# A hybrid decoder layer on one core: descriptor scratch of 4 KB, rows of inverse roots by two float32r products, and the norms of one k group four slots later

## The chip, the cores and the metric

The kernel runs on one core of a Trainium2 chip. The metric is the time of one execution on the device in microseconds, as the median of several runs. A profiled execution of the same program gives the trace. Its engines are TensorE (PE, with its weight loads shown apart as PEld), VectorE (DVE), ScalarE (ACT), GpSimd (POOL) and SyncE (SP); each takes its own queue of instructions in order. Transfers are issued by SyncE's queue (weights, transposes, results) and by GpSimd's (transfers that add to what lies at their target).

## The reference

One decoder layer for 512 tokens of 2048 channels, all in float32, with weights of 2048 x 7168, 1024 x 1024 and 2048 x 2048:

```python
h = rms_norm(x, norm_g)
a_val, a_glu, a_gate, q, k, v, b_gate = jnp.split(h @ w_in, SPLIT_POINTS, axis=-1)   # 1024 columns each
u = a_val * jax.nn.sigmoid(a_glu)
u = causal_depthwise_conv(u, conv_w, conv_b)                                      # 31 taps
u = jax.nn.silu(layer_norm(u, conv_norm_g, conv_norm_b))
y_a = (u @ conv_pw_w + conv_pw_b) * jax.nn.silu(a_gate)
q, k = rms_norm(q, q_norm_g), rms_norm(k, k_norm_g)                               # per head, 16 heads of 64
y_b = dilated_attention_mixture(q, k, v) * jax.nn.silu(b_gate)
out = x + jnp.concatenate([y_a, y_b], axis=-1) @ w_out
```

## The kernel before, in words

Activations lie with channels on the partitions and the 512 tokens along the free axis; q, k and v come out with tokens on the partitions. Weights come as *units* of 512 rows by 512 columns (1 MB), eight in flight (RING), and four (or fewer) units make a *group*: vg0 to vg3 (value and gate of the GLU), q0, k0, v0, bg0, q1, k1, v1, ag0, ag1, bg1, then the pointwise groups pw0 and pw1, then the output's wb and wa groups.

**Precision.** Almost every product is made of three float16 products (`tri`, L409 on): both operands are split into a high and a low float16 half, and high x high, high x low and low x high are summed. ScalarE rounds the high half (wh), VectorE subtracts it for the low half (wl). The first two groups (vg0, vg1) use a split into two float32r numbers instead (`exact_matmuls`, L876). Weights are scaled by a power of two; ScalarE finds a bound for it by squaring a whole unit into a tile that nobody reads (`junk`, in `row_squares`, L191) and summing, TensorE and VectorE sum it up, and GpSimd takes the inverse root by a power (`rsqrt`, L169, called from L205 on).

**Slots.** The order of all work is written by the program. A *slot* is a piece of TensorE's queue: six matmuls of 512 columns, eight slots to a unit. A calendar (`after(n, fn)`) puts work n slots ahead, and at each slot the program issues the work that is due, then convolution steps, then the matmuls. So the slot says where an instruction stands in each engine's queue, not when it runs.

**Seven products.** Groups vg3 and v0 (`SEVEN`) and the output's wa groups are computed as two by two blocks with seven products in place of eight. Such a group (`input_products`) needs sums of weight blocks: s1 is subtracted by VectorE, and s3, s2 and s4 (`BY_DMA`) are added by transfers from GpSimd's queue within the weights' own tiles (wf<-wf, L1119; in the output stage L933), 512 KB for each of two *pairs*. In a SEVEN group the program puts s2 at steps 3 and 4, s4 at 8 and 9; s2 reads what s3 made, s4 reads what s2 made, pair by pair. The step of a SEVEN group has 12 matmuls of 256 columns, and after its last step the next group's first weights are split (`split_hi`, `split_lo`). The transfers' descriptors lie in a scratch area whose size is an argument of the program, `dynamic_dma_scratch_size`.

**Convolution and layer norm.** The 31 taps run on VectorE as filler: at each slot `run_conv` issues convolution steps as long as VectorE's counted load stays under a pace, PACE before attention and PACE_2 once the first pair of heads has begun. The layer norm follows (`conv`, L534 on): a product with ones for the mean (L565), the centred squares, then `token_rsqrt` (L386 on), which makes a row of inverse roots by token on all partitions. It sums over channels with four small products (L390) into a column per 128 tokens, GpSimd takes the inverse roots of the 128 x 4 numbers, and the row has to be spread to all partitions. For the layer norm (n == C) this goes by DRAM: one transfer writes the 512 numbers (`by_token`, L396), a second reads them back to 128 partitions (`lnrow`, L397). For the first norm, over x, four diagonals are made on VectorE and one float32 product with ones gives the row (`rrow`, L400 to L406). Then, seven slots on, VectorE scales the eight channel tiles by the row (cv), ScalarE applies SiLU, and u is split for the pointwise products. The small products of the layer norm wait until a pair of heads is at least eight slots old.

**Norms of q and k.** `norm_qk` (L470 on) has four steps per tile of 128 tokens, at slots n after the tile has left PSUM: VectorE sums the squares by head (ss) and GpSimd takes the roots; VectorE scales z; ScalarE rounds the high half (qhl); VectorE subtracts, and SyncE's queue issues two transposing transfers. For k0 the steps of its four tiles fall around the start of v0, the SEVEN group behind it. Attention begins at the earliest 28 slots after k's last slot, at a multiple of eight slots from the start plus two.

## Time and profile before

| | |
|---|---|
| median of 3 runs | 831.17 us (830.96 to 832.64) |
| the profiled execution | 832.49 us |
| its span, first to last instruction | 830.6 us |
| granted clock of TensorE, mean | 0.997 |
| busy, share of the span: TensorE, VectorE, ScalarE, GpSimd | 98%, 83%, 66%, 15% |
| transfers | 122.71 MB, mean 148 GB/s |

All rows of the trace are of that one execution, and its times count from the span's start. A row of the timeline or the chain begins with the start in us and the length in us; in square brackets stand the engine's idle time before the instruction and what ended it. L80 is the line of a helper that all VectorE instructions go through, so they are told apart by their tiles. A row with x and a count is a group of instructions: busy time of all, mean of one in ns, and idle time ahead of them.

### The profile page before, as it was taken

What the parts mean: (1) busy time and instruction counts of PE and PEld (TensorE: products, weight loads), DVE (VectorE), ACT (ScalarE), POOL (GpSimd) and SP (SyncE); (2) the same over time, 40 slices, a digit from 0 to 9 for tenths busy, and PEclk for the clock granted to TensorE, in tenths of its full rate; (3) what the DMA queues carried; (4) which work ended last, traced back from release to release, by engine and by line L of the source; (5) the groups of instructions that cost most, each with busy time, mean ns of one, the idle gap of its engine ahead of it and who ended that gap; (6) DMA issues with size and microseconds to landing.
All of it is one profiled execution on the core that took longest, in us unless ns stands there. A gap on an engine that the chain in (4) does not pass through costs nothing.

```text
span 830.6 us, 13114 instructions
## 1 busy us (share of the span) xinstructions
PE 815.7 (98%) x5125; PEld 488.0 (59%) x5125; DVE 690.4 (83%) x1150; ACT 547.0 (66%) x768; POOL 124.2 (15%) x154
## 2 busy tenths in 40 slices
PE   9999999989999999999999999999998999999998
PEld 6787645854445864444444444444444444688887
DVE  6758989879897889999899898977367798888885
ACT  6667677465655579677666839578677948766541
POOL 0001022200514300003203010000210002232320
PEclk9999999999999999999999999999999999999999
DMA  9852243773392792627473642635344297579662
GB/s 339 336 209 102 101 128 77 138 217 109 107 193 55 148 253 102 165 102 165 133 151 113 163 128 79 149 101 155 102 109 120 92 225 249 125 173 190 115 123 69
DMA packets 95310, 122.71 MB, mean 148 GB/s; under 512 B 62416, under 2 KB 80592, under 8 KB 86032
## 3 DMA queue, kind: packets, MB, share of 16 engines
q1 hardware_dynamic: 80544, 107.37, 42.3%
q0 software_dynamic: 14416, 14.42, 12.2%
q8 instruction: 40, 0.66, 0.3%
q14 instruction: 22, 0.18, 0.1%
q10 hardware_dynamic: 288, 0.07, 0.0%
HBM read 88.82 MB, written 4.20 MB: 112 GB/s over the span
## 4 chain that ended last, share of the span: by engine, by line
PE 82%; DVE 5%; DMA 5%; issue 3%; ACT 2%; POOL 2%; SPq 0%; POOLq 0%; ACTq 0%; DVEq 0%
PE ps_l L411 21%; PE ps_l L413 21%; PE ps_l L412 21%; PE ps_l L876 10%; DMA wf<-wf 4%; PE ps_o L760 2%; PE ps_s L413 2%; PE ps_s L411 2%; PE ps_s L412 2%; PE ps_s L720 2%; DVE ws L80 1%; DVE wl L80 1%; DMA by_token<-lncol 1%; DVE cv L80 1%; ACT junk L191 1%
## 5 line engine op out<-in xcount | busy, mean ns | idle before, releaser
L80 DVE SCALAR_TENSOR_TENSOR cv<-u,cw,cv 128x511 f32<-128x511 f32 (+14 forms) x240 | 162.1, 730 | 1.0 <-ACT cv L541 1.0
L300 ACT ACTIVATE wh<-wf,ws 128x2048 f16<-128x2048 f32 x48 | 95.8, 1995 | 72.1 <-PE ps_l L412 72.1
L191 ACT ACTIVATE junk<-wf 128x2048 bf16<-128x2048 f32 x68 | 129.2, 1900 | 8.8 <-DMA wf<-w_dram 8.5
L80 DVE SCALAR_TENSOR_TENSOR wl<-wf,ws,wh 128x2048 f16<-128x2048 f32 x49 | 115.1, 2348 | 13.4 <-ACT wh L300 13.3
L413 PE MATMUL ps_l<-x,wl 128*128 128x512 f16 x320 | 121.4, 379 | 1.9 <-DVE wl L80 1.9
L412 PE MATMUL ps_l<-wl,x 128*128 128x512 f16 x320 | 121.3, 379 | 1.4 <-DVE wl L80 1.4
L411 PE MATMUL ps_l<-x,wh 128*128 128x512 f16 x320 | 121.4, 379 | 0.3 <-DVE glu L80 0.3
L411 PE MATMUL ps_l<-wh,x 128*128 128x512 f16 x320 | 121.4, 379 | 0.0
L413 PE MATMUL ps_l<-wh,x 128*128 128x512 f16 x320 | 121.3, 379 | 0.0
L412 PE MATMUL ps_l<-x,wh 128*128 128x512 f16 x320 | 121.3, 379 | 0.0
L80 DVE SCALAR_TENSOR_TENSOR ws<-wf,ws 128x1024 f16<-128x1024 f32 x56 | 71.4, 1278 | 11.9 <-ACT ws L1125 9.9
L413 PEld LDWEIGHTS <-wl 128*128 128x128 f16 x480 | 46.9, 98 | 58.0 <-DVE wl L80 4.6
L411 PEld LDWEIGHTS <-wh 128*128 128x128 f16 x480 | 47.0, 98 | 54.8 <-issue 3.3
L412 PEld LDWEIGHTS <-wh 128*128 128x128 f16 x480 | 46.9, 98 | 53.3 <-issue 3.6
L876 PE MATMUL ps_l<-xr,wr 128*128 128x512 f32 x288 | 70.7, 401 | 0.1
L876 PEld LDWEIGHTS ps_l<-xr,wr 128*128 128x128 f32 x288 | 54.6, 190 | 14.4 <-ACT xr L336 1.0
L413 PEld LDWEIGHTS <-x 128*128 128x128 f16 x368 | 36.0, 98 | 40.9 <-issue 2.7
L411 PEld LDWEIGHTS <-x 128*128 128x128 f16 x368 | 36.0, 98 | 39.5 <-issue 1.9
L205 POOL TENSOR_SCALAR ws<-ws 128x1 f32<-128x1 f32 x22 | 7.7, 349 | 339.4 <-DVE ws L80 338.8
L412 PEld LDWEIGHTS <-x 128*128 128x128 f16 x368 | 36.0, 98 | 37.0
L943 ACT ACTIVATE ws<-wf,ws 128x1024 f16<-128x1024 f32 x28 | 32.1, 1146 | 28.0 <-PE ps_l L413 10.6
L80 DVE TENSOR_TENSOR wr<-wf,wr 128x512 fp32r<-128x512 f32 x32 | 22.1, 691 | 24.0 <-ACT wr L286 23.9
(244 smaller groups left out, 1700.1 us busy)
## 6 DMA issues: line engine op xcount, KB each, us to landing
wf<-w_dram SPq DMA_DIRECT2D x72, 1024.0 KB, 5.1
wf<-wf POOLq DMA_DIRECT2D x24, 512.0 KB, 5.9
x<-xt_dram SPq DMA_DIRECT2D x16, 256.0 KB, 6.8
res<-xt_dram SPq DMA_DIRECT2D x8, 512.0 KB, 6.3
out_dram<-res SPq DMA_DIRECT2D x15, 256.0 KB, 2.8
wf<-w_dram SPq DMA_DIRECT2D x7, 512.0 KB, 7.2
wf<-wf POOLq DMA_DIRECT2D x6, 256.0 KB, 6.3
wf<-w_dram SPq DMA_DIRECT2D x2, 256.0 KB, 3.6
```

Source lines behind the costliest of these rows:

```text
L80: return getattr(self.engine, name)(out, src, *args, **kw)
L191: A.activation(junk[:, :n], src, AF.Square, scale=scale, accum_out=acc)
L205: G.tensor_scalar(scale, scale, 1e-30, 2.0 ** (-2 * top), op0=OP.max, op1=OP.mult)
L300: A.activation(parts[i][0], raw[i], AF.Copy, scale=wscale[units[i][3:]][0])
L411: T.matmul(ps, ah, bh, start=first, stop=False)
L412: T.matmul(ps, ah, bl, start=False, stop=False)
L413: T.matmul(ps, al, bh, start=False, stop=last)
L720: T.matmul(ps[i, a], qk["q", hf][q][rows, p4, i * P:w], qk["k", hf][k][rows, p4, :w], start=n == 0, stop=n == 2)
L760: T.matmul(po[rows, i * P:(i + 1) * P], vs[hf][j // 2][:, j % 2, 2 * p4 + a, vp * DH:(vp + 1) * DH], got["t", a][:, pp * (ALL // P) + FROM ...
L876: T.matmul(banks[group, m], wt[:, a, m * P:(m + 1) * P], xk[b], start=k == 0 and a == b == 0, stop=k == KC - 1 and a == 1)
L943: A.activation(t[:, 0], block(name), AF.Copy, scale=wscale["wa", g][0])
```

## The change

Six edits:

1. The descriptor scratch has 4096 bytes of each partition, where it had 2048.
2. `junk` has 8 bits an element, where it had 16: 2 KB of each partition less.
3. `token_rsqrt` makes the row for the layer norm as for the first norm, from diagonals on the chip; the two transfers by DRAM and their buffer are gone. In both, the diagonal is now split in two float32r parts, a rounded one and the rest, and two float32r products take the place of one float32 product.
4. In the layer norm the three pieces of `token_rsqrt` stand two slots apart, and the scaling follows two slots behind the last (six slots behind the sums, where it was seven). For the first norm the products stand at slot 36 in place of 35.
5. PACE_2 is 1380 in place of 1400.
6. The norms of k0 are put later: the sums of squares at slot 6 after the tile in place of 2, and the other steps at 10, 11 and 13 plus three slots per tile, where they were at 6, 7 and 9 plus four.

```diff
-PACE_2 = 1400
+PACE_2 = 1380
...
-    junk = const.tile([P, KU * S], BF16, name="junk")
+    junk = const.tile([P, KU * S], mybir.dt.uint8, name="junk")
...
         rsqrt(c)
-        if n == C:
-            by_token = dram.tile([S], F32, name="by_token")
-            G.dma_start(by_token.rearrange("(t p) -> p t", p=P), c)
-            G.dma_start(row, by_token.partition_broadcast(P))
-            return
         yield
-        diag = temp("diag")
+        diag = [temp("diag", R32) for _ in range(2)]
         for t in range(NT):
-            V.tensor_scalar(diag[:, t * P:(t + 1) * P], ident, c[:, t:t + 1], None, op0=OP.mult)
+            h, l = (d[:, t * P:(t + 1) * P] for d in diag)
+            V.tensor_scalar(h, ident, c[:, t:t + 1], None, op0=OP.mult)
+            V.scalar_tensor_tensor(l, ident, c[:, t:t + 1], h.bitcast(F32), op0=OP.mult, op1=OP.subtract)
         yield
         ps = s_ps.tile([P, S], F32, name="ps_s")
-        T.matmul(ps, ones, diag, start=True, stop=True)
+        for i, d in enumerate(diag):
+            T.matmul(ps, ones.bitcast(R32), d, start=i == 0, stop=i == 1)
         A.activation(row, ps, AF.Copy)
...
-        norm_qk(("k" if is_k else "q", half_i), z, sq, (2, 6 + 4 * t, 7 + 4 * t, 9 + 4 * t),
+        n = [2, 6 + 4 * t, 7 + 4 * t, 9 + 4 * t]
+        if is_k and ("v", half_i) in SEVEN:
+            n = [n[0] + 4] + [m + 4 - t for m in n[1:]]
+        norm_qk(("k" if is_k else "q", half_i), z, sq, n,
...
         for _ in token_rsqrt(acc2, C, LN_EPS, c, row):
-            pass
-        yield 7
+            yield 2
+        yield 2
...
-            for m in (32, 33, 35):
+            for m in (32, 33, 36):
...
-    nc = bacc.Bacc("TRN2", target_bir_lowering=False, num_devices=1, dynamic_dma_scratch_size=2048)
+    nc = bacc.Bacc("TRN2", target_bir_lowering=False, num_devices=1, dynamic_dma_scratch_size=4096)
```

Two places show what moves. The first is GpSimd's queue where v0 begins, before the change: after the two transfers of s3 stand the roots of k0's four tiles (ss with four numbers), the root of a weight scale (ws), and then the transfers of s2 (the last two rows; those of s4 follow):

```order
L478 TENSOR_SCALAR ss_2337<-ss_2337 128x8
L169 TENSOR_TENSOR ss_2337<-ss_2337,half_117 128x8
L478 TENSOR_SCALAR ss_2362<-ss_2362 128x8
L169 TENSOR_TENSOR ss_2362<-ss_2362,half_117 128x8
L478 TENSOR_SCALAR ss_2385<-ss_2385 128x8
L169 TENSOR_TENSOR ss_2385<-ss_2385,half_117 128x8
L205 TENSOR_SCALAR ws_2394<-ws_2394 128x1
L169 TENSOR_TENSOR ws_2394<-ws_2394,half_117 128x1
L478 TENSOR_SCALAR ss_2409<-ss_2409 128x8
L169 TENSOR_TENSOR ss_2409<-ss_2409,half_117 128x8
L1119 DMA wf_1793<-wf_1722 128x4x256
L1119 DMA wf_1936<-wf_1870 128x4x256
```

And the same place after it (line numbers there are three lower, and tiles have other numbers):

```order
L475 TENSOR_SCALAR ss_2364<-ss_2364 128x8
L168 TENSOR_TENSOR ss_2364<-ss_2364,half_115 128x8
L204 TENSOR_SCALAR ws_2395<-ws_2395 128x1
L168 TENSOR_TENSOR ws_2395<-ws_2395,half_115 128x1
L475 TENSOR_SCALAR ss_2384<-ss_2384 128x8
L168 TENSOR_TENSOR ss_2384<-ss_2384,half_115 128x8
L1119 DMA wf_1797<-wf_1726 128x4x256
L1119 DMA wf_1940<-wf_1874 128x4x256
L475 TENSOR_SCALAR ss_2407<-ss_2407 128x8
L168 TENSOR_TENSOR ss_2407<-ss_2407,half_115 128x8
```

The root of the third tile moved behind that of the weight scale, and that of the fourth moved behind the transfers of s2; the transfers of s4 follow it. On VectorE, two of the four sums of squares and the first scaling of z moved behind the low halves of v0's second block in the same way.

The second place is VectorE's queue at the layer norm. Before the change the scaling by the row (cv<-cv,lnrow) stands behind the root's input (lncol), a weight scale (ws, wi), the inverse denominators of both heads of a pair (st0, st1) and the sum for another scale:

```order
L80 TENSOR_SCALAR lncol_5671<-ps_s_5673 128x4
L80 TENSOR_SCALAR ws_5634<-ws_5634 128x1
L80 RECIPROCAL wi_5635<-ws_5634 128x1
L80 TENSOR_SCALAR st0_5552<-st0_5552 128x4
L80 RECIPROCAL st0_5552<-st0_5552 128x4
L80 TENSOR_SCALAR st1_5553<-st1_5553 128x4
L80 RECIPROCAL st1_5553<-st1_5553 128x4
L80 TENSOR_REDUCE ws_5726<-ps_s_5747 128x1
L80 TENSOR_TENSOR cv_1211<-cv_1211,lnrow_5672 128x512
```

After it, the eight instructions for the diagonals (the rounded part and the rest, four times; the first two are shown) come behind the weight scale, and the scaling ahead of the second head's denominators:

```order
L80 TENSOR_SCALAR lncol_5675<-ps_s_5677 128x4
L80 TENSOR_SCALAR ws_5638<-ws_5638 128x1
L80 RECIPROCAL wi_5639<-ws_5638 128x1
L80 TENSOR_SCALAR diag_5700<-ident_119,lncol_5675 128x128
L80 SCALAR_TENSOR_TENSOR diag_5701<-ident_119,lncol_5675,diag_5700 128x128
...
L80 TENSOR_SCALAR st0_5554<-st0_5554 128x4
L80 RECIPROCAL st0_5554<-st0_5554 128x4
L80 TENSOR_TENSOR cv_1215<-cv_1215,lnrow_5676 128x512
L80 TENSOR_SCALAR st1_5555<-st1_5555 128x4
L80 RECIPROCAL st1_5555<-st1_5555 128x4
```

The scaling moved up by two instructions and got eight new ones ahead of it. On TensorE the product for the mean stands 18 matmuls later than before, the four small products of the sums stand behind the same matmul, and the two new products 24 matmuls behind those; on ScalarE the copy of the row stands behind the exponentials of the pair's second head. SyncE's queue has the same order as before.

More of the change, by code (lines that the diff above doesn't have):

```diff
@@ L101, in layer @@
     s_ps = pool("s_ps", 8 - LP, space=PS)
-    dram = pool("dram", 1, space=bass.MemoryType.DRAM)
     ctx.enter_context(tc.manual_schedule())
```

## The prediction

> **What bounds the kernel now.** I read the page first, then who TensorE waited for, then its busy time by stretch, and then for each stretch with idle time the queue and the chain behind it. The page's head:

> ```profile
> span 830.6 us, 13114 instructions
> PE 815.7 (98%) x5125; PEld 488.0 (59%) x5125; DVE 690.4 (83%) x1150; ACT 547.0 (66%) x768; POOL 124.2 (15%) x154
> ```

> TensorE is busy in 815.7 of 830.6 us, so only what shortens its own work or its 14.9 us of idle time can be seen in the result. The waits of TensorE, in us in total, number of times and longest, say where most of that is:

> ```profile
> PE ps_l L411 <- ACT u L312: 2.6, 1, 2.6
> PE ps_l L413 <- DVE wl L80: 1.9, 2, 1.1
> PE ps_l L413 <- DVE ws L80: 1.7, 2, 0.9
> PE ps_l L412 <- DVE ws L80: 1.6, 3, 0.8
> PE ps_l L412 <- DVE wl L80: 1.4, 1, 1.4
> PE ps_s L147 <- POOL wz L144: 1.0, 1, 1.0
> PE ps_l L411 <- ACT ws L1125: 0.8, 1, 0.8
> PE ps_l L412 <- DVE u L80: 0.4, 1, 0.4
> PE ps_l L411 <- DVE glu L80: 0.3, 1, 0.3
> ```

> They add to 11.7 us; 1.0 of it is the start, and the remaining 3.2 us of the 14.9 come after the last product. The busy times by stretch place the rest (the first number after the length is TensorE's busy time, the third VectorE's; the last three are the granted clock, the share of the DMA engines and GB/s):

> ```profile
> 173.00:181.00 8.00, 4.89 (x37) 3.28 (x36) 6.38 (x7) 6.94 (x6) 0.00 (x0) 1.00 0.57 210
> 264.00:304.00 40.00, 37.28 (x334) 32.22 (x332) 31.69 (x39) 23.90 (x27) 12.37 (x12) 1.00 0.84 184
> 304.00:608.00 304.00, 304.00 (x1834) 142.18 (x1832) 256.78 (x482) 215.47 (x323) 33.40 (x48) 1.00 0.47 128
> 608.00:629.00 21.00, 16.45 (x86) 7.14 (x85) 17.17 (x29) 16.62 (x26) 1.22 (x3) 0.98 0.63 163
> 629.00:827.40 198.40, 198.40 (x1551) 141.34 (x1547) 166.16 (x264) 123.87 (x176) 36.58 (x44) 0.99 0.61 147
> ```

> So TensorE idles 3.11 us at the end of group vg3, 2.72 us in and behind v0 (both computed with seven products), and 4.55 us where the pointwise products begin: 10.4 us in all. Between and behind these places it never waits.

> **The larger scratch.** GpSimd's timeline shows the accumulating transfers of vg3 (the first four; s2 of pair 0 and 1, then s4 of both) and a pair in the output stage:

> ```profile
> 145.27 1.34 POOL L1119 DMA_DIRECT2D wf<-wf  x1 [0.33 <-issue]
> 151.08 1.31 POOL L1119 DMA_DIRECT2D wf<-wf  x1 [4.47 <-DMA wf<-wf]
> 157.26 1.29 POOL L1119 DMA_DIRECT2D wf<-wf  x1 [4.86 <-DMA wf<-wf]
> 163.34 1.31 POOL L1119 DMA_DIRECT2D wf<-wf  x1 [4.79 <-DVE cv L80]
> ...
> 728.83 2.52 POOL L933 DMA_DIRECT2D wf<-wf  x2 [4.94 <-issue]
> ```

> Four transfers of 512 KB are issued about 6 us apart, each when the one before has landed, though s2 of pair 1 depends on nothing of pair 0. At 728.83 a transfer of 512 KB and one of 256 KB go out back to back. I read this as room in the scratch for more than one 512 KB transfer but not for two; twice the scratch then holds two, and by the pair's 768 KB three. In the chain of waits stand the second s2 and the second s4 of vg3, and the second s4 of v0, with the time from issue to landing:

> ```profile
> 151.08 5.86 DMA wf<-wf
> ...
> 163.34 9.96 DMA wf<-wf
> ...
> 288.61 7.95 DMA wf<-wf
> ```

> s4 of pair 1 lands at 173.30; ScalarE splits it (ws), VectorE splits it (ws) and then q0's first weights (wl), and these three are what TensorE waits for between 173 and 181. With room, s2 of pair 1 follows s2 of pair 0 by its 1.3 us of issue, at 146.6. s4 waits for the s2 of its own pair to land: pair 0 at 151.1, as its copy lands now. If the engines took the two transfers strictly one after the other, the second s2 would land at 157 as it does now, s4 of pair 1 would go out at 157 instead of 163.34 and land at 163 to 167 even if it took the 9.96 us of today. That is at least 6 us earlier than today, and the waits it feeds sum to 3.11 us. **Term: -3.1 us.**

> In v0 the same four transfers stand, and the last landed at 296.56. Of the 2.72 us there, the longest waits for ws and wl, 0.8 and 1.1, hang on it in the same way. With room it goes out as much earlier as in vg3, 6 us or more. **Term: -1.9 us.**

> **The norms of k0, four slots on.** A slot of plain products is six matmuls. These are the chain's piece for one, and the first wait of TensorE in v0:

> ```profile
> 587.96 0.22 PE ps_l L412
> ...
> 269.03 0.27 PE L412 MATMUL ps_l<-ws,tx 128*128 128x256 f16 x1 [0.63 <-DVE ws L80]
> ```

> A slot is thus 1.3 us. The product at 269.03 waits for VectorE's split of v0's second block; ahead of that split VectorE has done four reductions of squares and one scaling, each of this price:

> ```profile
> L80 DVE TENSOR_TENSOR z<-z,ss 128x512 f32<-128x512 f32 x16 | 10.9, 682 | 0.0
> ```

> Now two of the reductions and the scaling come behind it, and ScalarE's rounding of the first tile too. Three times 0.68 us exceed the 0.63 us. **Term: -0.6 us.** What is moved costs elsewhere. GpSimd's root of the third tile still stands ahead of s2 of pair 0, and its reduction is now later on VectorE: I put that transfer about 1 us later than today, and the fourth tile's root now stands between s2 and s4, where GpSimd waits for a landing anyway. VectorE's subtraction s1 of pair 1 needs the second s2, which by this lands only about 1 us earlier than today, and the displaced scalings stand around it. TensorE, 0.6 us ahead by then, needs s1's split 0.6 us sooner, where it waited 0.2 us already. I take a wait of 0.5 us in place of 0.2. **Term: +0.3 us.** The transposes on SyncE's queue move with the norms, in the same order among the weight loads; the last tile's norm is one slot later, and the first scores of attention are over ten slots behind it, so this costs nothing; without that gap a slot would be 1.3 us.

> **The rows of inverse roots.** For the layer norm, the present path is seen in TensorE's sums, in GpSimd's roots (the first of them for another scale, ahead of this one), in the way by DRAM, on ScalarE and on VectorE (rows of the timeline, those of the transfers and of the first root from the chain):

> ```profile
> 590.84 0.95 PE L390 MATMUL ps_s<-ones,lnacc 128*128 128x2 f32 x8
> ...
> 590.31 2.42 POOL ws L169
> ...
> 592.98 1.02 POOL L169 TENSOR_TENSOR lncol<-lncol,half 128x4 f32<-128x4 f32 x1
> ...
> 594.37 8.55 DMA by_token<-lncol
> ...
> 603.49 4.00 DMA lnrow<-by_token
> ...
> 597.73 0.80 ACT L732 ACTIVATE sx<-sx,st,sc 128x512 f32<-128x512 f32 x1
> ...
> 607.51 0.69 DVE L80 TENSOR_TENSOR cv<-cv,lnrow 128x512 f32<-128x512 f32 x1 [6.41 <-DMA lnrow<-by_token]
> ```

> VectorE stood 6.41 us at the first scaling by the row, and the splits of weights and of u that TensorE waits for from 608 to 629 were queued behind it. In the new form the diagonals need eight small instructions, and then two products:

> ```profile
> L80 DVE TENSOR_SCALAR diag<-ident,rstd 128x128 f32<-128x128 f16 x4 | 0.9, 279 | 1.1 <-POOL rstd L169 1.1
> L80 DVE SCALAR_TENSOR_TENSOR hl<-sx,st,hl 128x128 f16<-128x128 f32 x16 | 5.5, 344 | 0.5 <-ACT hl L743 0.5
> ...
> 56.09 0.86 PE ps_s L405 x2
> ...
> 65.37 16.88 PE ps_l L876 x72
> ```

> Four at 0.28 and four at no more than 0.34 make 2.5 us at most, from the root's end at 594.0 to 596.5. The products stand four slots behind the four small products of the sums (which end near 591.8), so at 591.8 + 4 x 1.3 = 597.0: VectorE is done first, by 0.5 us. ScalarE copies the row after its exponential of 597.73 to 598.5, so VectorE has it at 599.2 instead of 607.5. The whole tail moves up by some 8 us where TensorE was 4.55 us late. **Term: -4.6 us**; what is then late next is nothing that I find, since from 601 to 607 VectorE only stood. TensorE's own work: a float32r product is 16.88/72 = 0.23 us, the old float32 one 0.86. At the start that is 0.47 for 0.86, and at the layer norm 0.47 is new. **Term: +0.1 us.** At the start the row also comes one slot later and VectorE gets four more small instructions, at most 1.4 us; VectorE is idle before several of its steps there, and the 0.3 us wait for glu is the only one that could grow. Bounds 0 to 0.7; I take **+0.1 us**, near the lower end because VectorE's next use of the row follows an instruction that waits for ScalarE anyway.

> **Edits priced at nothing.** The throwaway squares go to 8 bits. No row has such an output; the nearest two are the same operation to 32 and to 16 bits:

> ```profile
> L345 ACT ACTIVATE xsq<-x 128x512 f32<-128x512 f32 x15 | 9.1, 615 | 0.0
> L191 ACT ACTIVATE junk<-gate 128x512 bf16<-128x512 f32 x12 | 7.5, 629 | 17.2 <-DVE gate L80 17.2
> ```

> They differ by 2%; that much either way on 68 large squares is under 3 us of an engine that is idle for a third of the span, and 0 to 0.3 us on the path. The slower pace takes convolution steps out of VectorE's slots from about 305 on; TensorE does not wait there at all, VectorE has 47 us free of 304, the mean's product comes three slots later, and the sums of the layer norm stand behind the same matmul as before, since they wait for the end of a head pair's scores in both. If that cover were gone, three slots would be 3.9 us.

> **The sum.** -3.1 - 1.9 - 0.6 + 0.3 - 4.6 + 0.1 + 0.1 = -9.7 us. The profiled execution took 832.49 us, 1.9 more than its span, and the median of the runs is 831.17, so 1.3 us less than the profiled one. From the median: 831.2 - 9.7 = 821.5 us.

> **The rivals.**

> *The scratch is not what spaces the transfers.* If the queue handles one 512 KB transfer at a time whatever its room, vg3 and v0 keep 3.1 and 1.9 us. For it: the third and fourth issue of vg3 also depend on landings. Against: the pair at 728.83. The time is 831.2 - 9.7 + 5.0 = 826.5. Chance 0.12.

> *The row is late in another way.* TensorE takes its queue in order, so a diagonal that is late stops it, and what I gave as cover is 0.5 us. If the root came 2 us later (the one ahead of it on GpSimd took 2.4 us), TensorE would stand 1.5 us at once and VectorE's row would still be 6 us earlier than now: 823. With a convolution that ends later as well, up to 825. Chance 0.10.

> *Transfers together hold up the weight loads: slower.* The 9.96 us of s4 in vg3 against the 5.86 of the s2 before it shows that loads and accumulating transfers slow each other, by 4.1 us. In the output stage each of the four groups issues several of the latter; were weight loads late by 4.1 us in each of them, with nothing left to hide it, 16.4 us would come on top: 831.2 - 9.7 + 16.4 = 837.9. It decides from 2.4 us a group. For it: the DMA share of 0.61 there. Against: in 198.4 us TensorE does not wait once although 768 KB go out together there already, and the bytes to be moved stay the same. Chance 0.03. [...]

> *Gains that are given back.* New waits of the same size in v0 and at the pointwise start, through reordered VectorE steps: within 0.2% (1.7 us, about what a measurement of this kernel can tell from no change) of 831.2. Chance 0.03.

> **The numbers.** The forecast has 0.72. Its own bounds: all 10.4 us and the 0.3 us of glu gone and nothing new gives 820.4; 1 us more of new waits than I took, with the late glu at its bound, gives 823. The range must take in the first two rivals: 820 to 827 leaves out the slow end and what is unforeseen. Faster 0.94, same 0.03, slower 0.03.

> **What would show it.** In the profile after: s2 of pair 1 issued within 2 us of pair 0 in vg3 (if 6 us, the first rival holds); no TensorE wait near 173 to 181 and at most 1 us in v0; VectorE's first scaling by the row less than 10 us behind the root of lncol, without an idle of several us before it; no wait for u or wl where the pointwise products begin; the float32r products of L402 with no wait ahead of them. The prediction is wrong if TensorE's idle sum stays above 6 us, or if its busy time changes by more than 1 us.

## The result and the profile after

The changed kernel takes **822.73 us** (median of 4 runs, 822.14 to 823.46); the kernel before took 831.9 us beside it (4 runs, 830.96 to 833.15). The ratio is 0.9889, with a 95% interval from 0.9872 to 0.9907: faster by 9.2 us, where the prediction had 9.7 less and 821.5 us. The profiled execution took 823.46 us.

The page's head and TensorE's waits (in us in total, number of times, longest):

```profile
span 821.7 us, 13129 instructions
PE 814.4 (99%) x5127; PEld 488.3 (59%) x5127; DVE 693.3 (84%) x1162; ACT 547.6 (67%) x769; POOL 124.8 (15%) x152
```

```profile
PE ps_l L409 <- DVE ws L80: 2.0, 1, 2.0
PE ps_s L146 <- POOL wz L143: 1.0, 1, 1.0
PE ps_l L410 <- DVE wl L80: 0.5, 1, 0.5
PE ps_l L408 <- DVE glu L80: 0.3, 1, 0.3
```

The waits add to 3.8 us instead of 11.7. All of vg3's and of the pointwise start's are gone; what is left beside the start and the 0.3 us for glu, which stay, is in v0, and the largest of it, 2.0 us, is new. GpSimd's timeline in vg3 shows both s2 transfers going out as one pair, then s4 twice:

```profile
145.41 2.68 POOL L1119 DMA_DIRECT2D wf<-wf  x2 [0.27 <-issue]
151.72 1.29 POOL L1119 DMA_DIRECT2D wf<-wf  x1 [3.63 <-DMA wf<-wf]
155.43 1.28 POOL L1119 DMA_DIRECT2D wf<-wf  x1 [2.42 <-DMA wf<-wf]
```

The last s4 goes out 7.9 us earlier on the trace's scale (155.43 for 163.34). At the layer norm stand GpSimd's root, the first and last diagonal on VectorE, the two products and the first scaling:

```profile
590.09 1.02 POOL L168 TENSOR_TENSOR lncol<-lncol,half 128x4 f32<-128x4 f32 x1
...
591.14 0.29 DVE L80 TENSOR_SCALAR diag<-ident,lncol 128x128 fp32r<-128x128 f16 x1 [0.63 <-POOL lncol L168]
...
593.22 0.35 DVE L80 SCALAR_TENSOR_TENSOR diag<-ident,lncol,diag 128x128 fp32r<-128x128 f16 x1
...
593.75 0.82 PE L402 MATMUL ps_s<-diag,ones 128*128 128x512 f32 x2
...
596.25 0.69 DVE L80 TENSOR_TENSOR cv<-cv,lnrow 128x512 f32<-128x512 f32 x1 [2.39 <-ACT lnrow L403]
```

From the root's end at 591.11 to the scaling are 5.1 us; before, the scaling stood 13.5 us behind the root (594.00 to 607.51).

When the same product starts in both traces tells where the time went (after minus before, in us, of each part alone; the prediction's terms beside it):

| part | predicted | measured |
|---|---|---|
| start: the rows by two products, the row a slot later | -0.3 (-0.39 and +0.1) | -0.46 |
| end of vg3 | -3.1 | -3.61 |
| v0 to its last wait at 304 | -2.2 (-1.9 - 0.6 + 0.3) | **+1.19** |
| the layer norm's two products | +0.47 | +0.46 |
| pointwise start, 608 to 632 | -4.6 | **-6.91** |
| last product | -9.7 | -9.33 |

The total is right by luck, because two misses nearly cancel: v0 came out 3.4 us worse than its terms, and the pointwise start 2.3 us better. One thing stands behind both that I did not foresee, and the granted clock shows it (the column behind POOL's). First the kernel before, behind its wait for u, then the kernel after, behind its new wait in v0:

```profile
624.00:628.00 4.00, 0.99 (x5) 0.24 (x3) 1.84 (x3) 3.18 (x7) 0.00 (x0) 1.00 0.98 290
628.60:629.60 1.00, 1.00 (x26) 1.00 (x22) 0.80 (x2) 1.00 (x3) 0.00 (x0) 0.50 0.00 0
...
632.00:633.00 1.00, 1.00 (x8) 0.31 (x4) 0.42 (x1) 1.00 (x2) 0.00 (x0) 1.00 0.00 0
```

```profile
283.00:284.00 1.00, 1.00 (x8) 0.79 (x7) 1.00 (x2) 0.56 (x2) 0.00 (x0) 0.66 1.24 181
284.00:285.00 1.00, 1.00 (x7) 0.70 (x5) 1.00 (x2) 0.44 (x1) 0.00 (x0) 0.50 1.19 144
285.00:286.00 1.00, 1.00 (x7) 0.69 (x6) 0.72 (x1) 1.00 (x2) 0.00 (x0) 0.50 1.08 399
286.00:287.00 1.00, 1.00 (x7) 0.78 (x6) 0.74 (x1) 0.23 (x1) 0.00 (x0) 0.63 1.08 410
287.00:288.00 1.00, 1.00 (x12) 0.89 (x10) 1.00 (x2) 0.00 (x0) 0.00 (x0) 1.00 0.83 257
```

TensorE runs at half clock for about 3.4 us behind each (in v0 7 or 8 products in a microsecond instead of 12), and counts as fully busy. By the same products' starts that costs 1.57 us before at 628 to 632 and 1.6 us after at 283 to 287: the first is most of the surplus of the pointwise start, the second more than the whole loss in v0.

### The profile page after: what moved, and what is told of

The parts are those of the page before. It is cut to its first block, busy times and chain, and to the rows that moved or that the text cites. A ratio compares the mean times of both kernels' runs of the same rounds, so it can differ in the third digit from the quotient of the medians.

```text
span 821.7 us, 13129 instructions
## 1 busy us (share of the span) xinstructions
PE 814.4 (99%) x5127; PEld 488.3 (59%) x5127; DVE 693.3 (84%) x1162; ACT 547.6 (67%) x769; POOL 124.8 (15%) x152
## 4 chain that ended last, share of the span: by engine, by line
PE 93%; DVE 3%; DMA 2%; issue 1%; ACT 1%; POOL 0%; ACTq 0%; POOLq 0%; DVEq 0%
PE ps_l L408 24%; PE ps_l L410 24%; PE ps_l L409 24%; PE ps_l L876 10%; PE ps_s L410 2%; PE ps_s L408 2%; PE ps_s L409 2%; PE ps_s L720 2%; PE ps_o L760 2%; DMA wf<-wf 1%; DMA wf<-w_dram 1%; DVE ws L80 1%; DVE wl L80 1%; PE ps_s L146 0%; DVE z L80 0%
## 5 line engine op out<-in xcount | busy, mean ns | idle before, releaser
L80 DVE SCALAR_TENSOR_TENSOR cv<-u,cw,cv 128x511 f32<-128x511 f32 (+14 forms) x240 | 161.7, 728 | 0.0
L190 ACT ACTIVATE junk<-wf 128x2048 uint8<-128x2048 f32 x68 | 129.2, 1900 | 12.3 <-DMA wf<-w_dram 12.0
L80 DVE SCALAR_TENSOR_TENSOR wl<-wf,ws,wh 128x2048 f16<-128x2048 f32 x49 | 115.1, 2349 | 19.8 <-ACT wh L299 19.7
L80 DVE SCALAR_TENSOR_TENSOR ws<-wf,ws 128x1024 f16<-128x1024 f32 x56 | 71.3, 1278 | 10.2 <-ACT ws L1125 7.8
L876 PE MATMUL ps_l<-xr,wr 128*128 128x512 f32 x288 | 70.2, 400 | 0.0
L204 POOL TENSOR_SCALAR ws<-ws 128x1 f32<-128x1 f32 x22 | 10.1, 460 | 363.1 <-DVE ws L80 334.1
L876 PEld LDWEIGHTS ps_l<-xr,wr 128*128 128x128 f32 x288 | 54.5, 190 | 13.9 <-ACT xr L335 0.9
L732 ACT ACTIVATE sx<-sx,st,sc 128x128 f32<-128x128 f32 (+1 forms) x64 | 40.9, 640 | 0.4 <-DVE st L80 0.3
```

Of the source, the lines that this page charges most:

```text
L80: return getattr(self.engine, name)(out, src, *args, **kw)
L190: A.activation(junk[:, :n], src, AF.Square, scale=scale, accum_out=acc)
L204: G.tensor_scalar(scale, scale, 1e-30, 2.0 ** (-2 * top), op0=OP.max, op1=OP.mult)
L732: A.activation(xi, xi, AF.Exp, scale=sc, bias=neg[a][:, i:i + 1], accum_out=total[a][:, i:i + 1])
L876: T.matmul(banks[group, m], wt[:, a, m * P:(m + 1) * P], xk[b], start=k == 0 and a == b == 0, stop=k == KC - 1 and a == 1)
```

## The experiments

The theory at this point: the scratch removes vg3's waits, the layer norm's row the pointwise start's, and the moved norms cost something in v0. Except where said, each kernel is the changed one with the edit shown. Times are medians, of 4 to 10 runs, with the kernel before timed on the same chip.

**The scratch at 2 KB again.**

```diff
-    nc = bacc.Bacc("TRN2", target_bir_lowering=False, num_devices=1, dynamic_dma_scratch_size=4096)
+    nc = bacc.Bacc("TRN2", target_bir_lowering=False, num_devices=1, dynamic_dma_scratch_size=2048)
```

> The changed kernel with the scratch of before (2 KB), all else as changed. Theory (room in the scratch spaced the transfers): in vg3 the four transfers of s2 and s4 stand some 6 us apart again, the waits of 3.1 us between 173 and 181 return (3.6 us of TensorE's progress, by the two traces), and in v0 the second s2 lands 1 to 2 us later than the 278.5 of the changed kernel, which lengthens the wait of 2.0 us before s1's products: 826 to 830 us in all. Rival (the queue takes one such transfer at a time whatever its room, and something else closed the waits of vg3): no change against the changed kernel's 822.7 us, within 1 us.

829.63 us (828.51 to 830.10), ratio 0.9975 (0.9964 to 0.9986): the scratch is worth 6.9 us here. GpSimd's issues in vg3 are 6 us apart again, and waits are back: in vg3 two of the three, 1.3 and 0.9 us, and in v0 one of 4.2 us with the half clock behind it (0.52, 0.50, 0.50 and 0.77 in the four microseconds from 288 on). The mean clock of the profiled run, 0.996, is worth some 6.6 us at half clock, so about two such stretches:

```profile
144.20 1.34 POOL L1119 DMA_DIRECT2D wf<-wf  x1 [0.33 <-issue]
150.01 1.30 POOL L1119 DMA_DIRECT2D wf<-wf  x1 [4.47 <-DMA wf<-wf]
155.93 1.29 POOL L1119 DMA_DIRECT2D wf<-wf  x1 [4.62 <-DMA wf<-wf]
161.95 1.30 POOL L1119 DMA_DIRECT2D wf<-wf  x1 [4.73 <-DVE cv L80]
```

```profile
PE ps_l L409 <- DVE ws L80: 4.4, 2, 4.2
...
PE ps_l L408 <- ACT ws L1125: 1.3, 1, 1.3
...
PE ps_l L410 <- DVE ws L80: 0.9, 1, 0.9
```

The room in the scratch does space the transfers; the first rival falls.

**The scratch alone, in the kernel before.** The 4.2 us exceed anything that the kernel before waited in v0, so the 6.9 us might hold more than the scratch's own worth.

```diff
-    junk = const.tile([P, KU * S], BF16, name="junk")
+    junk = const.tile([P, KU * S], mybir.dt.uint8, name="junk")
...
-    nc = bacc.Bacc("TRN2", target_bir_lowering=False, num_devices=1, dynamic_dma_scratch_size=2048)
+    nc = bacc.Bacc("TRN2", target_bir_lowering=False, num_devices=1, dynamic_dma_scratch_size=4096)
```

> The kernel before with the scratch of 4 KB alone (and the squares' scrap as bytes, which makes the room for it). Taken out of the changed kernel, the scratch was worth 6.9 us, but there the later norms had moved work behind the late transfers: the kernel without it idled 4.16 us before the z products of v0 and ran 3.4 us at half clock behind that, where the kernel before waited 1.9 us in all. Theory: the scratch alone is worth what vg3 shows (3.6 us) and what v0 shows without the norms' cost (about 1 to 2 us), so 831.9 - 5.1 = 826.8, from 826 to 827.5; the rest of the 6.9 is an interaction with the norms. Rival: the parts add up, so that the scratch alone gives 831.9 - 6.9 = 825.0. In both the waits of 610 to 628 us and the stretch at half clock behind them stay.

827.11 us (826.84 to 828.85), ratio 0.9947 (0.9933 to 0.9960), 4.4 us of 832 with an interval from 3.3 to 5.6: the interaction is there. The trace tells more than the time. vg3's waits are gone, but v0 waits 3.0 us in all, no less than the 2.7 of the kernel before; by the same products' starts v0 loses 0.2 us. Its later waits have another cause. On ScalarE:

```profile
288.58 1.91 ACT L191 ACTIVATE junk<-wf 128x2048 uint8<-128x2048 f32 x1 [4.23 <-DMA wf<-w_dram]
290.40 0.19 ACT L191 ACTIVATION_READ_ACCUMULATOR junk<-wf 128x1 bf16 x1
290.49 2.17 ACT L1125 ACTIVATE ws<-wf,ws 128x1024 f16<-128x1024 f32 x2
```

The squares that measure the next weight tile (junk) wait for its load, and the splits of z's weights (ws) are queued behind them. In the kernel before the last s4 landed later still, at 296.56, and hid this.

**The layer norm's row by DRAM again.**

```diff
+        if n == C:
+            by_token = dram.tile([S], F32, name="by_token")
+            G.dma_start(by_token.rearrange("(t p) -> p t", p=P), c)
+            G.dma_start(row, by_token.partition_broadcast(P))
+            return
...
-            yield 2
-        yield 2
+            pass
+        yield 7
```

> The changed kernel with the layer norm's row by DRAM and its seven slots as before; the first norm keeps its two products. Theory (the row's way cost both the waits and a stretch at half clock behind them): waits of 4 to 5 us return where the pointwise products begin, a stretch of some 3 us at clock 0.50 follows, 828 to 830 us. Rival (only the waits count, and the products cost what they take): 826 to 827.5 us, with the clock at 1.00.

828.73 us (828.42 to 830.54), ratio 0.9970 (0.9958 to 0.9982): the row is worth 6.0 us, 1.4 more than the term of 4.6. The waits are back (4.1 us of them), and the half clock behind them, in the profiled run, one of the two slowest of ten, for twice as long as in the kernel before (623.3 to 630.1):

```profile
PE ps_l L414 <- ACT u L312: 2.6, 1, 2.6
...
PE ps_l L416 <- DVE ws L80: 0.8, 1, 0.8
```

```profile
624.00:625.00 1.00, 0.80 (x2) 0.20 (x2) 1.00 (x2) 1.00 (x2) 0.00 (x0) 0.50 0.76 320
...
629.00:630.00 1.00, 1.00 (x10) 0.29 (x6) 0.35 (x1) 1.00 (x3) 0.00 (x0) 0.50 0.00 0
```

**The norms of k0 at their old slots.**

```diff
-        if is_k and ("v", half_i) in SEVEN:
-            n = [n[0] + 4] + [m + 4 - t for m in n[1:]]
```

> The changed kernel with the norms of k0 at their slots of before. Theory (the wait of 2.0 us before s1's products in v0 comes from the moved norms, which put a third root ahead of s2 on GpSimd and two reductions and scalings around s1 on VectorE): that wait falls under 0.5 us, TensorE's clock stays at 1.00 after it, the wait of 0.6 us for v0's second block returns: 819.5 to 821.5 us. Rival (the wait comes from the second s2 in any case, since TensorE arrives 4 us earlier): it stays at 1.5 us or more and the time is 822 to 824 us.

821.20 us (820.91 to 821.39), ratio 0.9880 (0.9862 to 0.9897). No run of it is as slow as the fastest of the changed kernel (822.14): moving the norms costs 1.5 us at the median. The first row is the 0.62 us for v0's second block, which the move was worth, and another 0.53 for z; the 2.0 us before s1's products are gone:

```profile
PE ps_l L409 <- DVE ws L80: 1.2, 2, 0.6
...
PE ps_l L410 <- DVE wl L80: 1.0, 1, 1.0
```

What the 2.0 us were, VectorE's timeline of the changed kernel shows. The subtractions s1 of pair 0 and 1 (wf) wait for the two s2 transfers to land; a scaling of k0 (z) and a sum (cb) follow, and then the split that TensorE waits for (ws, at 280.85):

```profile
274.36 1.23 DVE L80 TENSOR_TENSOR wf<-wf 128x1024 f32<-128x1024 f32 x1 [3.14 <-DMA wf<-wf]
...
278.51 1.22 DVE L80 TENSOR_TENSOR wf<-wf 128x1024 f32<-128x1024 f32 x1 [1.13 <-DMA wf<-wf]
279.65 0.69 DVE L80 TENSOR_TENSOR z<-z,ss 128x512 f32<-128x512 f32 x1
280.25 0.68 DVE L80 SCALAR_TENSOR_TENSOR cb<-ps_l,cb 128x512 f32<-128x512 f32 x1
280.85 1.28 DVE L80 SCALAR_TENSOR_TENSOR ws<-wf,ws 128x1024 f16<-128x1024 f32 x1
```

GpSimd's timeline, of the changed kernel and of the one with the old slots, gives the reason for the late landing. With the moved norms the third tile's root ends just ahead of the pair and the fourth tile's follows; with the old slots the fourth tile's is done by then. The roots themselves start later: their sums come four slots later, GpSimd starts on the first at 259.55 in place of 253.37, and then works them off almost without a pause.

```profile
265.95 2.57 POOL L168 TENSOR_TENSOR ss<-ss,half 128x8 f32<-128x8 f32 x1
268.48 2.67 POOL L1119 DMA_DIRECT2D wf<-wf  x2
270.13 1.26 POOL L475 TENSOR_SCALAR ss<-ss 128x8 f32<-128x8 f32 x1
```

```profile
263.68 2.52 POOL L168 TENSOR_TENSOR ss<-ss,half 128x8 f32<-128x8 f32 x1
266.15 2.67 POOL L1117 DMA_DIRECT2D wf<-wf  x2
```

So the pair goes out 2.3 us later with the moved norms (268.48 for 266.15), though one root less stands ahead of it.

**s1 of pair 1 two slots later,** so that the subtraction that waits for the second transfer no longer stands ahead of pair 0's split.

```diff
-                 ((-8, "s3", 0), (-7, "s3", 1), (3, "s2", 0), (4, "s2", 1), (8, "s4", 0), (9, "s4", 1), (9, "s1", 0), (11, "s1", 1))]
+                 ((-8, "s3", 0), (-7, "s3", 1), (3, "s2", 0), (4, "s2", 1), (8, "s4", 0), (9, "s4", 1), (9, "s1", 0), (13, "s1", 1))]
```

> The changed kernel with the subtraction s1 of pair 1 at step 13 in place of 11 in the SEVEN groups, so that VectorE makes the low half of pair 0 before it stands at the second s2's landing. Theory (VectorE's queue order is what makes TensorE wait 2.0 us before s1's products in v0): that wait is under 0.3 us, no half clock behind it, 819 to 820.5 us. Rival (the block is late whatever stands ahead of it, because the first s2 lands late): the wait stays above 1 us, 822 to 823 us.

822.12 us (821.81 to 822.32), ratio 0.9891 (0.9873 to 0.9909): the theory's time was missed, and the rival's was met without its wait of over 1 us. Pair 0's wait is gone, but pair 1 now waits 0.7 us, and the waits behind it grow:

```profile
PE ps_l L409 <- DVE ws L80: 1.8, 2, 1.1
...
PE ps_l L410 <- DVE wl L80: 1.0, 1, 1.0
```

The 1.1 and 1.0 are z's and wl's, behind ScalarE's measuring squares again. What a step ahead saves is waited for there.

**The pace as it was.**

```diff
-PACE_2 = 1380
+PACE_2 = 1400
```

> The changed kernel with the one constant PACE_2 at 1400 again. The prediction priced this edit at nothing, so this theory gives 822.7 us within 0.5, with the same idle time before s1's products (1.97 us) and the stretch at half clock behind it. A rival: the constant moves the transfers of the next parts near v0 and takes the 1.97 us or the stretch at half clock away or lengthens it; then 821 or less, or 824 or more.

823.47 us (822.14 to 824.47), ratio 0.9899 (0.9884 to 0.9913), beside 823.23 for the unchanged kernel measured again (below): no difference that these runs can tell, though 0.7 us above the first value and thus just outside what was expected. In the profiled run the wait was 2.1 us long and no half clock followed. All four runs show a mean clock of 1.0, and their spans still lie between 820.4 and 822.7 us: something other than the half clock moves the runs as well, and what it is stays open.

**Later measuring squares, with the old norms.** If the squares are the next cover, they have to move behind the split of z. To the edit of the old norms comes:

```diff
-MEASURE = 8
+MEASURE = 11
```

> The changed kernel with the norms of k0 at their old places (821.2 us as measured) and the squares that measure a new weight tile in groups of seven products at 11 slots behind the load instead of 8. In v0 ScalarE then doesn't stand at the weight load ahead of the split of z's high half: the wait of 0.53 us there and part of the 0.98 us before the products with wl go, so 820.2 us, from 819.8 to 820.7. Rival: the wait on the returned block and on VectorE's half wl end at the same time as before, since VectorE and not ScalarE is late there; then 821.2 within 0.4.

**819.51 us** (819.24 to 819.57), ratio 0.9851 (0.9838 to 0.9865): faster than both kernels, and by more than expected, since both waits go, not one and a part. TensorE waits for nothing after v0's second block:

```profile
PE ps_s L146 <- POOL wz L143: 1.0, 1, 1.0
PE ps_l L409 <- DVE ws L80: 0.6, 1, 0.6
PE ps_l L408 <- DVE glu L80: 0.3, 1, 0.3
```

ScalarE's row shows how: only one split of z stands behind the squares now, and the rounding of the next weight (wh) comes 1.3 us sooner (291.21 with the old norms alone).

```profile
282.74 2.18 ACT L1123 ACTIVATE ws<-wf,ws 128x1024 f16<-128x1024 f32 x2
286.99 1.91 ACT L190 ACTIVATE junk<-wf 128x2048 uint8<-128x2048 f32 x1 [2.07 <-DMA wf<-w_dram]
288.81 0.19 ACT L190 ACTIVATION_READ_ACCUMULATOR junk<-wf 128x1 bf16 x1
288.90 1.13 ACT L1123 ACTIVATE ws<-wf,ws 128x1024 f16<-128x1024 f32 x1
289.94 1.99 ACT L299 ACTIVATE wh<-wf,ws 128x2048 f16<-128x2048 f32 x1
```

The two waits that go add to 1.51 us, and the products behind them come 1.83 us earlier: each wait costs some 0.16 us more than its idle time.

**Later squares with the moved norms, and the changed kernel again.**

> The changed kernel with the later measuring squares alone (11 slots instead of 8); the norms of k0 stay four slots on. Theory: the wait before s1's products comes from VectorE's queue and not from these squares, so about 2 us of waiting there stay, while the wait for wl (0.47 us) goes with its 0.16 us of refilling: 822.1, from 821.3 to 822.8, and single runs lie over 1 us apart, since in some executions a stretch at half clock follows the wait. Rival: the squares were what made v0 late, so that this gives nearly the 819.5 us of the version with the old norms.

> The changed kernel as it is, beside the one with the later squares on the same chip: 822.7 us as before, and by every theory the same waits; whether the stretch at half clock follows the wait before s1's products may differ from run to run, with about 1.5 us between runs that have it and runs that don't.

821.78 us (820.43 to 823.08), ratio 0.9877 (0.9856 to 0.9898), and 823.23 us (822.83 to 823.44), ratio 0.9889 (0.9874 to 0.9904). The squares were not what made s1's products late, so the rival falls: the wait stays, 1.98 us in the profiled run. The two waits of 1.0 us behind it, which the unchanged kernel's profile has, are gone. The single runs are the clearest look at the half clock (each run's span and mean granted clock):

```
later squares, moved norms:  818.7 at 1.0    818.8 at 1.0    821.2 at 0.998  821.3 at 0.998
changed kernel, first call:  820.3 at 1.0    820.9 at 0.999  821.0 at 0.999  821.7 at 0.998
changed kernel, again:       821.0 at 1.0    821.3 at 1.0    821.6 at 0.998  821.7 at 1.0
later squares, old norms:    817.5 at 1.0    817.6 at 1.0    817.7 at 1.0    817.8 at 1.0
```

Half clock for 3.4 us is 0.2% of the span's clock, so 0.998 is one such stretch (0.999 is less than one: in the profile of the kernel before, the clock falls once more behind the last product, 1.1 us before the span's end, at 829.50, and that alone is 0.07%). The same program has it in two executions of four, and is then 2.5 us slower. Without it the moved norms still cost 1.1 us (818.7 for 817.6). In the changed kernel itself the difference is smaller and less clean: its profile with the stretch has a wait of 0.5 us behind it, a profile without it has two of 1.0, so that part of what the stretch takes was lost anyway, and one run of 821.7 has none. The 1.5 us that were expected between its runs are not seen.

## Why the prediction was right, and where it was not

**vg3: right in mechanism and nearly in size.** -3.61 for -3.1. The s2 pair went out within 2.7 us, s4 of pair 1 goes out 7.9 us earlier where I had "at least 6", and all three waits went. The rest of the size is three waits at about 0.16 us each beyond their idle time, as measured above.

**v0, the scratch's second term: failed.** The step was "the longest waits for ws and wl, 0.8 and 1.1, hang on it in the same way", -1.9. The scratch alone left 3.0 us of waiting in v0 where there were 2.7. By the same products' starts the term measured +0.2 us in place of -1.9. s4 of pair 1 did go out over 6 us earlier: 277.36 for 288.61, 7.3 us on the products' scale. The transfer was what came last, but the next one, ScalarE's splits behind squares that wait for a weight load, was as late. I asked what is late next at the pointwise start, and not here. Moving those squares takes the waits away, with the norms at their old slots and at their new ones, which shows the cover.

**v0, the norms: one half right, the other mis-sized.** The 0.6 us for the second block went as predicted (0.62 returns with the old slots). "I take a wait of 0.5 us in place of 0.2" measured 1.97 us. I had seen both causes, the root ahead of the pair and the scalings around s1, and sized both too small. On the products' scale (the trace after is 4.08 us ahead there) the pair goes out 2.1 us later than before the change (268.48 for 270.43), where I had about 1. VectorE starts on what the second transfer brings 0.56 us later (278.51 for 282.03), where I had it land 1 us earlier. And a scaling of z, 0.60 us of VectorE's queue, now stands between that subtraction and the split. With the 0.62 us by which TensorE is ahead and the 0.20 that it waited already, these add to 1.98 us; 1.97 were measured. Then comes the half clock. The edit as a whole, a gain of 0.3 us in the sum, was a loss of 1.5 us at the median.

**The layer norm's row: right, and larger.** The diagonals took 2.4 us for "2.5 at most", the products went without a wait, the scaling came 5.1 us behind the root's end, and every wait at the pointwise start went. The cover for the diagonals was 0.2 us or less (VectorE ends at 593.57, the products start at 593.75), where I had 0.5. That the term was -6.91 and not -4.6 is 1.57 us of half clock that went with the waits, and what each wait costs beyond its idle time; the experiment puts it at 6.0 us at the median.

**What was named as proof against.** TensorE's busy time was to change by no more than 1 us, and changed by 1.3 (815.7 to 814.4). The busy time is no measure of the work where the clock changes: in the profile with the later squares and the old norms, whose mean clock is 1.0, it is 811.9, for the same 5127 products as the 814.4 of the changed kernel. Two more of the named signs came: v0 waited 2.4 us where I had at most 1, and the idle time, by the page's head 7.3 us (821.7 - 814.4; 3.8 of it are waits, most of the rest lies behind the last product), stayed above 6. By its own signs the prediction was wrong; v0 and the half clock brought them, and the good total hides it.

**The rivals.** The first fell by the experiment on the scratch. The late row didn't occur. Transfers together did no harm in the output stage: TensorE's products there start 9.32 us earlier at its beginning and 9.33 at its end. Given back, as the fourth rival had it, was a part, in v0 alone.

## What to carry to other kernels

When a wait is removed, look up what else the waiting instruction's engine has ahead of it, and when that ends; a sum of the waits that a late transfer ends last is an upper bound, not a term. Small steps that are put later also put later what stands behind them in a queue that keeps its order: the pair of transfers had one root less ahead of it and still went out 2.3 us later. A wait of 2 us cost 3.6 where the half clock followed (1.97 of waiting, 1.6 behind it), so a long wait can be worth more than several short ones of the same sum; behind the waits of 2.0 and 2.1 us in two other profiles (below) it didn't follow. A kernel's spread between runs can be the sign of it: of the 19 runs of the kernel before beside the first experiments, the five with a mean clock of 1.0 took 829.8 to 831.2 us, the fourteen below it 830.3 to 834.1, and the best version's four, all at 1.0, lie 0.3 us apart. It is no proof: the four runs with the old pace, all at 1.0, lie 2.3 us apart.

## What the runs showed of the hardware

| kernel and place | waits, us | clock behind it |
|---|---|---|
| before, pointwise start | 2.60 and 0.41 | 0.50 |
| scratch alone, pointwise start | 2.6 | 0.50 |
| scratch at 2 KB again, v0 | 4.2 | 0.50 |
| changed kernel, v0 | 1.97 | 0.50 |
| row by DRAM, pointwise start | 2.6, then 0.2 | 0.50, twice as long |
| changed kernel again, v0 | 1.83 | 1.00 |
| old pace, v0 | 2.1 | 1.00 |
| later squares, moved norms, v0 | 1.98 | 1.00 |
| before, vg3 | 0.75, 0.93 and 1.43 | 1.00 |

So the length of a wait alone does not decide: behind 1.97 us the clock fell, behind 1.98 and 2.1 it did not. What else decides is not shown here, and neither is why one program has the stretch in some executions only (with the later squares and the moved norms, two of four runs have a mean clock of 0.998 and two of 1.0). In the first half of the stretch of 6.8 us TensorE idled 0.9 us, in the four single ones 0.3 us or less. The clock falls behind the last product too: in the kernel before at 829.50, 197.97 us after it had returned, in the changed kernel at 822.6, 535.9 us after it. These are 58 and 157 times the 3.41 us; what ties them to that length is not shown.

Two accumulating transfers of 512 KB in flight together land about 4 us apart (in v0 VectorE starts on them at 274.36 and 278.51); one after the other they went out 6 us apart. With a scratch of 2 KB one of them went out at a time, with 4 KB two. ScalarE's squares took 1.90 us with eight-bit output as with sixteen-bit.
